# Attention scores on one core: the first set transposed in twelve pieces, and the later twelve output tiles stored two by two

## The chip, the cores and the metric

The kernel runs on one core of a Trainium2 chip. The metric is the device time of one execution in microseconds, given as the median of several executions. A profile is one further execution, recorded instruction by instruction; its own time stands beside its span (from the first to the last recorded instruction) in the table below.

The core has four engines that appear in this text: TensorE (PE in the profile, PEld for its weight loads), VectorE (DVE), ScalarE (ACT) and GpSimd (POOL). SyncE (SP) computes nothing here; its queue (SPq) issues transfers. Transfers (DMA) are carried by 16 engines of their own, called lanes here.

## The reference

```python
def setup_inputs():
    batch, heads, seq, dim = 8, 8, 512, 64
    q, k: float32 [8, 8, 512, 64]

def reference(q, k):
    scale = 1.0 / np.sqrt(q.shape[-1])
    return (np.einsum('bhqd,bhkd->bhqk', q, k) * scale).astype(np.float32)
```

Sixty-four products of 512x64 by 64x512 are formed. The inputs are 16.8 MB together, the float32 output is 67.1 MB, so most of what moves is output.

## The kernel before

**Tiles.** The output is cut into 16 tiles of 4 MB (`ALL = 16`, index `g`). A tile lives in one of four SBUF buffers, `bigs[g % 4]`, each 128 partitions by 2 halves `x` by 8 rows `i` by 512 columns in float32. A tile is made in four quarters, numbered `n = 0..3`: quarter `n` is half `x = n // 2`, rows `i = 0..3` (low) or `4..7` (high). One quarter is four matmuls, each 128x512, into four of the eight PSUM banks `ps[:, i]`, followed by one 128x2048 instruction that multiplies by the scale and writes PSUM to the buffer. The low quarters always use banks 0 to 3 and the high ones banks 4 to 7, so quarter 2 has to wait until quarter 0 has been read out, and quarter 3 until quarter 1 has.

**Sets.** Two consecutive tiles, `2b` and `2b + 1`, use one set `b` of transposed operands. `kT` and `qz` have room for two sets, `b % 2`. A set is made by VectorE from `xb` with two transposes of keys (`turn_keys`, 64x1024) and four of queries (`turn_queries`, 32x1024). Before it makes set `b`, VectorE waits until TensorE has finished with set `b - 2` (`pe >= 8 * (b - 1)`, line 183).

**Loads and casts.** The inputs arrive in seven 2 MB loads and two of 1 MB, into the same four `bigs` buffers that later hold output. GpSimd casts them to bfloat16 into `xb` (line 113), one unit `v` of four after the other, and gives `ready` one count for each cast half-unit.

**Who waits for what.** All order is set by semaphores that are written out by hand; there is no scheduler at work.

- TensorE runs one loop of four iterations over tiles `t = 0..3` (lines 123 to 148). The dictionary `waits` says ahead of which matmul `(x, i)` it waits, and `takes` lowers a semaphore again. A tile's second matmul, `(0, 1)`, waits until the buffer is free. The last matmuls of every second tile, from `(1, 6)` on, wait for the next set: `waits[1, 6] = (f"set{1 - two}", 1)` (line 135).
- ScalarE reads out all 64 quarters in order (lines 151 to 156) and gives `act0`/`act1`, or `out` for a tile's last quarter.
- SyncE, in order, waits for `out`, gives `freed0`/`freed1` to TensorE, and issues the 4 MB store (lines 82 to 88). Each buffer has a semaphore of its own, `store0` to `store3`, which the 16 lanes raise by one each when their share of the store has landed.

Of the kernel before, what the change touches and what calls it, by code (L numbers as in the profile page):

```python
# [5 lines left out]
def kernel(  # L6
# [5 lines left out]
    nc = tc.nc  # L12
    B, H, S, D = q.shape
    scale = 1.0 / (D ** 0.5)
    P = 128
    Q = 32
    UNITS = B // 2
    G = H // 2
# [3 lines left out]
    RO = 8  # L22
    JJ = J // RO
    W = 4
    ALL = 2 * B
    SETS = 2 * UNITS
    SLOTS = UNITS - 1

    f32 = mybir.dt.float32
# [1 line left out]

    names = ["ready", "zeroed", "turned", "pe", "out", "act0", "act1", "freed0", "freed1", "set0", "set1"]
    sem = {name: nc.alloc_semaphore(name) for name in names}
    load_sems = [nc.alloc_semaphore(f"load{n}") for n in range(2 * UNITS)]
    halves = [load_sems[0], nc.alloc_semaphore("load0b")]
    store_sems = [nc.alloc_semaphore(f"store{n}") for n in range(UNITS)]

# [1 line left out]
    q_r = q.rearrange("(v b) (x s h) (m j) d -> v (s h m) (b x) (j d)", b=2, x=2, s=2, j=R)  # L43
    k_r = k.rearrange("(v b) (x s h) (m j) d -> v (s h m) (b x) (j d)", b=2, x=2, s=2, j=R)
    k_0 = k.rearrange("(v b) (x s h) (m j) d -> v b (s h m) x (j d)", b=2, x=2, s=2, m=Q)[0]
    out_r = out.rearrange("(v b) (x s h) (u i) k -> v s b (h u) x (i k)", b=2, x=2, s=2, i=RO)


    bigs = [nc.alloc_sbuf_tensor(f"big{n}", [P, 2, RO, S], f32)[:] for n in range(UNITS)]
    xb = nc.alloc_sbuf_tensor("xb", [P, 2 * SLOTS, J, D, 2], bf16)[:]  # L50
    kT = nc.alloc_sbuf_tensor("kT", [P, 2 * G, S], bf16)[:]
    qz = nc.alloc_sbuf_tensor("qz", [P, 2 * G, RO, P], bf16)[:]
    ps = nc.alloc_psum_tensor("ps", [P, RO, S], f32)[:]

    xw = xb.rearrange("p n w d e -> p n (w d e)").bitcast(f32).rearrange(
        "p n (w d) -> p n w d", d=D)
    kw = kT.bitcast(f32)
    qw = qz.bitcast(f32)

    def xf(v):  # L60
        return bigs[v].rearrange("p x i k -> p (x i k)").rearrange("p (x s c) -> p x s c", x=2, s=2)

    def slot(v, x):
        return v % SLOTS * 2 + x
# [3 lines left out]
    for s, queue in enumerate((nc.sync, nc.scalar)):  # L68
        first_load = queue.dma_start(
            out=xf(0)[:, 0, s].rearrange("p (x c) -> p x c", x=2), in_=k_0[s]  # L70
# [4 lines left out]

    for n in range(1, 2 * UNITS):
        v, x = divmod(n, 2)
        nc.sync.dma_start(out=xf(v)[:, x].rearrange("p s c -> p (s c)"), in_=(k_r, q_r)[x][v]  # L80
                          ).then_inc(load_sems[n], 16)
    for g in range(ALL):
        nc.sync.wait_ge(sem["out"], g + 1)
        if g < ALL - 1:
            nc.sync.sem_inc(sem[f"freed{g // 2 % 2}"], 1)  # L85
        nc.sync.dma_start(out=out_r[g // 4, g // 2 % 2, g % 2],
                          in_=bigs[g % UNITS].rearrange("p x i k -> p x (i k)")
                          ).then_inc(store_sems[g % UNITS], 16)
    for n in range(UNITS):
        nc.sync.wait_ge(store_sems[n], 16)  # L90

    for v in range(UNITS):
        if v == SLOTS:
            nc.gpsimd.wait_ge(sem["turned"], 1)
            nc.gpsimd.sem_inc(sem["set1"], 1)
        for x in range(2):
            if v or x:
                nc.gpsimd.wait_ge(load_sems[2 * v + x], 16)  # L100
            for s in range(2):
                if v == x == 0:
                    nc.gpsimd.wait_ge(halves[s], 16)
                src = xf(v)[:, x, s]
                dst = xb[:, slot(v, x)]
                if x == 0:
                    src = src.rearrange("p (w e d) -> p w e d", e=2, d=D)
                    dst = dst[:, s * J // 2:(s + 1) * J // 2].rearrange("p w d e -> p w e d")
                else:
                    src = src.rearrange("p (jj e i d) -> p jj e i d", e=2, i=RO, d=D)  # L110
                    dst = dst.rearrange("p (i jj) d e -> p jj e i d", i=RO)[
                        :, s * JJ // 2:(s + 1) * JJ // 2]
                cast = nc.gpsimd.tensor_copy(out=dst, in_=src)  # L113
            cast.then_inc(sem["ready"], 1)
        nc.gpsimd.wait_ge(sem["ready"], 2 * v + 2)
        nc.gpsimd.sem_inc(store_sems[v], 16)

# [1 line left out]
    pe = nc.tensor  # L121
    pe.wait_ge(sem["set0"], 1)
    with pe.Fori(0, ALL // 4):
        for t in range(4):
            two, r = divmod(t, 2)
            was = (t + 3) % 4
            waits = {(0, 0): (f"act{was // 2}", was % 2 * 3 + 3), (0, 1): (f"store{t}", 16),
                     (0, W): (f"freed{was // 2}", was % 2 + 1),
                     (1, 0): (f"act{two}", 3 * r + 1), (1, W): (f"act{two}", 3 * r + 2)}
            takes = {(1, 1): (f"store{t}", 16)}  # L130
            if r == 0:
                takes |= {(0, 5): (f"act{1 - two}", 6), (0, 6): (f"freed{1 - two}", 2),
                          (1, 2): (f"set{two}", 1)}
            else:
                waits[1, 6] = (f"set{1 - two}", 1)
            every = sem | {f"store{n}": store_sems[n] for n in range(UNITS)}
            for x in range(2):
                for i in range(RO):
                    if (x, i) in waits:
                        name, count = waits[x, i]  # L140
                        pe.wait_ge(every[name], count)
                    ins = pe.matmul(out=ps[:, i], lhsT=qz[:, 2 * t + x, i], rhs=kT[:, 2 * t + x],  # L142
                                    start=True, stop=True)
                    if i % W == W - 1:
                        ins.then_inc(sem["pe"], 1)
                    elif (x, i) in takes:
                        name, count = takes[x, i]
                        ins.then_inc(every[name], -count)


    for g in range(ALL):
        for n in range(4):
            x, i = n // 2, n % 2 * W
            nc.scalar.wait_ge(sem["pe"], 4 * g + n + 1)
            freed = nc.scalar.mul(out=bigs[g % UNITS][:, x, i:i + W], in_=ps[:, i:i + W], mul=scale)  # L155
            freed.then_inc(sem["out" if n == 3 else f"act{g // 2 % 2}"], 1)

    def turn_keys(b, y):  # L160
        s = b % 2 * 2 * Q
        out = kw[2 * y * Q:2 * (y + 1) * Q, b % 2 * G:(b % 2 + 1) * G]
        if b < 2:
            out = out.rearrange("d g (m w) -> d g w m", m=Q)
        else:
            out = out.rearrange("d g (m w) -> d w m g", w=J)
        return nc.vector.transpose(  # L167
            out=out, in_=xw[s:s + 2 * Q, slot(b // 2, 0), :, y * Q:(y + 1) * Q])

    def turn_queries(b, y, h):  # L170
        s = (b % 2 * 2 + h) * Q
        d = (2 * y + h) * Q
        return nc.vector.transpose(  # L173
            out=qw[d:d + Q, b % 2 * G:(b % 2 + 1) * G, :, h * Q:(h + 1) * Q].rearrange(
                "d g i (m jj) -> d i jj m g", jj=JJ),
            in_=xw[s:s + Q, slot(b // 2, 1), :, y * Q:(y + 1) * Q].rearrange(
                "p (i jj) d -> p i jj d", i=RO))

    nc.vector.memset(qz, 0.0).then_inc(sem["zeroed"], 1)  # L179
    nc.vector.wait_ge(sem["zeroed"], 1)  # L180
    for b in range(SETS):
        if b >= 2:
            nc.vector.wait_ge(sem["pe"], 8 * (b - 1))
        if b % 2 == 0:
            nc.vector.wait_ge(sem["ready"], b + 1)
        for y in range(2):
            last = turn_keys(b, y)
            if b == 0:
                last.then_inc(sem[("act1", "freed1")[y]], (6, 2)[y])
        if b % 2 == 0:  # L190
            nc.vector.wait_ge(sem["ready"], b + 2)
        for y in range(2):
            for h in range(2):
                last = turn_queries(b, y, h)
        last.then_inc(sem["turned" if b == 1 else f"set{b % 2}"], 1)
    nc.vector.sem_inc(sem["set0"], 1)


# [28 lines left out]
```

## Time and profile before

| quantity | value |
|---|---|
| time, median of 10 executions | 200.9 us (200.72 to 201.04) |
| the profiled execution: its time, and its span | 200.76 us, 199.2 us |
| TensorE busy | 86.0 us, 256 matmuls |
| VectorE busy | 99.3 us |
| ScalarE busy | 116.3 us, 64 quarters read out |
| GpSimd busy | 38.9 us |
| HBM read and written | 16.78 MB, 67.11 MB; 421 GB/s over the span |
| granted TensorE clock, mean | 0.807 of full speed |

The profile's busy times are sums over the whole span, and no engine reaches 60% of it. The row of the DMA is a different matter: it has its own line of forty slices, and the time from issue to landing of a store contains the time that it stands in its queue. A transfer's landing is the moment at which all of its lanes have raised its semaphore.

### The profile page before, as it was taken

To read this page: it belongs to the slowest core of one execution; us is meant where nothing else is said; L and a number is where in the kernel's file an instruction comes from. 1 tells how busy PE (TensorE), PEld (TensorE's weight loads), DVE (VectorE), ACT (ScalarE), POOL (GpSimd) and SP (SyncE) were. 2 spreads that over 40 slices of the span, in tenths; PEclk is the share of its full clock that TensorE was granted. 3 is DMA by queue.
4 is the path that set the end of the run, shared out by engine and by line. 5 is a ranking of instruction groups with operands and counts; after the bars stand their busy time and mean duration, and the time that the engine had idled before them with its cause. 6 is when DMAs were issued, how large, how long until landed. Compare 5 with 4: busy or idle time off the path is not lost.

```text
span 199.2 us, 742 instructions
## 1 busy us (share of the span) xinstructions
PE 86.0 (43%) x256; PEld 24.4 (12%) x256; DVE 99.3 (50%) x49; ACT 116.3 (58%) x65; POOL 38.9 (20%) x20
## 2 busy tenths in 40 slices
PE   0000076555566557556555555566657672000000
PEld 0000021111111111111111111121212120000000
DVE  4247999799699599139904990598000000000000
ACT  2000039999999949594959595949595959000000
POOL 0499999797000000000000000000000000000000
PEclk9999999999999966696979797858585869555555
DMA  5999999999999999999999999999999999999997
GB/s 204 428 454 434 428 421 421 421 415 431 434 434 421 438 428 434 434 421 434 431 438 434 420 434 434 428 434 424 431 438 424 438 424 434 434 425 424 421 424 316
DMA packets 5905, 83.90 MB, mean 421 GB/s; under 512 B 400, under 2 KB 400, under 8 KB 912
## 3 DMA queue, kind: packets, MB, share of 16 engines
q1 hardware_dynamic: 5632, 82.84, 97.6%
q10 hardware_dynamic: 272, 1.05, 1.3%
q14 instruction: 1, 0.01, 0.0%
HBM read 16.78 MB, written 67.11 MB: 421 GB/s over the span
## 4 chain that ended last, share of the span: by engine, by line
DMA 49%; ACT 24%; DVE 4%; PE 4%; POOL 2%; issue 0%; SPq 0%
DMA out_dram<-big 43%; ACT big L155 24%; DMA big<-in_q_dram 6%; DVE qz L173 4%; PE ps L142 4%; POOL xb L113 2%; SPq L85 0%
## 5 line engine op out<-in xcount | busy, mean ns | idle before, releaser
L155 ACT ACTIVATE big<-ps 128x2048 f32<-128x2048 f32 x64 | 115.0, 1910 | 50.7 <-PE ps L142 50.6
L142 PE MATMUL ps<-kT,qz 128*128 128x512 bf16 x256 | 86.0, 474 | 80.5 <-DVE qz L173 26.2
L173 DVE STREAM_TRANSPOSE qz<-xb 32x1024 f32<-32x1024 f32 x32 | 64.5, 2015 | 1.5 <-POOL xb L113 1.1
L167 DVE STREAM_TRANSPOSE kT<-xb 64x1024 f32<-64x1024 f32 x16 | 31.3, 1959 | 34.9 <-PE ps L142 28.3
L142 PEld LDWEIGHTS ps<-kT,qz 128*128 128x128 bf16 x256 | 24.4, 112 | 141.6 <-ACT big L155 55.1
L113 POOL CAST xb<-big 128x2048 bf16<-128x2048 f32 x16 | 38.6, 2475 | 9.3 <-DMA big<-in_k_dram 7.5
L179 DVE MEMSET qz<- 128x4096 uint32 x1 | 3.5, 3472 | 2.9 <-PEq L74 2.9
L155 ACT ACT_TABLE_LOAD x1 | 1.3, 1283 | 2.0 <-PEq L74 2.0
L211 POOL MEMSET const-float32-0.0<- 128x1 f32 x1 | 0.1, 98 | 0.2 <-issue 0.2
L211 POOL MEMSET const-bfloat16-1.0<- 128x1 bf16 x1 | 0.1, 101 | 0.0
L211 POOL MEMSET const-uint8-127<- 128x1 uint8 x1 | 0.1, 101 | 0.0
L211 POOL MEMSET const-float32-1.0<- 128x1 f32 x1 | 0.1, 98 | 0.0
## 6 DMA issues: line engine op xcount, KB each, us to landing
out_dram<-big SPq DMA_DIRECT2D x16, 4096.0 KB, 30.1
big<-in_q_dram SPq DMA_DIRECT2D x4, 2048.0 KB, 23.8
big<-in_k_dram SPq DMA_DIRECT2D x3, 2048.0 KB, 23.8
big<-in_k_dram SPq DMA_DIRECT2D x1, 1024.0 KB, 7.1
big<-in_k_dram ACTq DMA_DIRECT2D x1, 1024.0 KB, 8.7
```

What stands on the lines that cost most here:

```text
L113: cast = nc.gpsimd.tensor_copy(out=dst, in_=src)
L142: ins = pe.matmul(out=ps[:, i], lhsT=qz[:, 2 * t + x, i], rhs=kT[:, 2 * t + x], start=True, stop=True)
L155: freed = nc.scalar.mul(out=bigs[g % UNITS][:, x, i:i + W], in_=ps[:, i:i + W], mul=scale)
L167: return nc.vector.transpose(out=out, in_=xw[s:s + 2 * Q, slot(b // 2, 0), :, y * Q:(y + 1) * Q])
L173: return nc.vector.transpose(out=qw[d:d + Q, b % 2 * G:(b % 2 + 1) * G, :, h * Q:(h + 1) * Q].rearrange("d g i (m jj) -> d i jj m g", jj=J ...
L179: nc.vector.memset(qz, 0.0).then_inc(sem["zeroed"], 1)
L211: nc = _bacc.Bacc("TRN2", target_bir_lowering=False, num_devices=1)
```

## The change

Three things change in the order of work, and one in who does it.

1. **The first set in 12 pieces.** Set 0 was made with 2 key and 4 query transposes. It is now made with 4 key transposes (half the heads each) and 8 query transposes (half the rows each). TensorE is released (`set0`) after the first four query pieces, and its high quarters wait for the other four.
2. **The first stores.** Stores of tiles 0 to 2 wait for TensorE (`pe >= 4 * g + 6`, that is, both quarters of the next tile's first half written) in place of ScalarE's `out`, and SyncE gives TensorE no counts for them.
3. **Pairs.** Tiles 4 to 15 are stored two by two: six stores of 8 MB in place of twelve of 4 MB. The four buffers become one tensor `big`, and the semaphores `store0..3` become `free0` and `free1`, one for each pair of buffers. TensorE waits for a free buffer only at the first tile of a pair, for both buffers at once. SyncE gives its count (`high0`/`high1`) once for each pair, after the store is issued.
4. **Quarter 1 by VectorE.** For tiles 4 to 15 quarter 1 is read out by VectorE (`tensor_scalar_mul`, 128x2048 from PSUM), 12 of the 64; ScalarE keeps 52. These 12 stand at fixed places in VectorE's order: for sets 3 to 7, two key transposes, quarter 1 of tile `2b - 2`, two query transposes, quarter 1 of tile `2b - 1`, two query transposes, then the count for the set. The last two tiles' come at the end.

The counts `act` and `freed` become `low` and `high`, one for each half of the PSUM banks.

```diff
-    for g in range(ALL):
-        nc.sync.wait_ge(sem["out"], g + 1)
-        if g < ALL - 1:
-            nc.sync.sem_inc(sem[f"freed{g // 2 % 2}"], 1)
-        nc.sync.dma_start(out=out_r[g // 4, g // 2 % 2, g % 2],
-                          in_=bigs[g % UNITS].rearrange("p x i k -> p x (i k)")
-                          ).then_inc(store_sems[g % UNITS], 16)
+    for g in range(ALL):
+        if g < UNITS - 1:
+            nc.sync.wait_ge(sem["pe"], 4 * g + 6)
+        elif g % 2:
+            nc.sync.wait_ge(sem["out"], (g - UNITS + 3) // 2)
+        else:
+            continue
+        dst = out_r[g // 4, g // 2 % 2]
+        free = sem[f"free{g // 2 % 2}"]
+        if g < UNITS:
+            nc.sync.dma_start(out=dst[:, g % 2 * 2:g % 2 * 2 + 2],
+                              in_=bigs[g].rearrange("p x i k -> p x (i k)")).then_inc(free, 16)
+        else:
+            nc.sync.dma_start(out=dst, in_=big[:, g % UNITS - 1:g % UNITS + 1].rearrange(
+                "p n x i k -> p (n x) (i k)")).then_inc(free, 32)
+        if UNITS - 1 <= g < ALL - 1:
+            nc.sync.sem_inc(sem[f"high{g // 2 % 2}"], 1)
...
-            waits = {(0, 0): (f"act{was // 2}", was % 2 * 3 + 3), (0, 1): (f"store{t}", 16),
-                     (0, W): (f"freed{was // 2}", was % 2 + 1),
-                     (1, 0): (f"act{two}", 3 * r + 1), (1, W): (f"act{two}", 3 * r + 2)}
+            was = (f"{two}", 2) if r else (f"{1 - two}", 4)
+            waits = {(0, 0): ("low" + was[0], was[1]), (0, W): ("high" + was[0], was[1]),
+                     (1, 0): (f"low{two}", 2 * r + 1), (1, W): (f"high{two}", 2 * r + 1)}
             if r == 0:
+                waits[0, 1] = (f"free{two}", 32)
...
             else:
-                waits[1, 6] = (f"set{1 - two}", 1)
+                waits |= {(0, 1): ("ready", 2 * t + 2), (1, 6): (f"set{1 - two}", 1)}
...
+    def evacuate(g, n):
+        x, i = n // 2, n % 2 * W
+        by_vector = g >= UNITS and n == 1
+        engine = nc.vector if by_vector else nc.scalar
+        engine.wait_ge(sem["pe"], 4 * g + n + 1)
+        to, src = bigs[g % UNITS][:, x, i:i + W], ps[:, i:i + W]
+        if by_vector:
+            freed = nc.vector.tensor_scalar_mul(out=to, in0=src, scalar1=scale)
+        else:
+            freed = nc.scalar.mul(out=to, in_=src, mul=scale)
...
+    nc.vector.wait_ge(sem["ready"], 1)
+    for n in range(2):
+        for y in range(2):
+            last = turn_keys(0, y, slice(2 * n, 2 * n + 2))
+    last.then_inc(sem["low1"], 4)
+    nc.vector.wait_ge(sem["ready"], 2)
+    for n in range(RO // W):
+        for y, h in sides:
+            last = turn_queries(0, y, h, slice(n * W, (n + 1) * W))
+        last.then_inc(sem[("set0", "high1")[n]], (1, 4)[n])
+    for b in range(1, SETS):
         if b >= 2:
             nc.vector.wait_ge(sem["pe"], 8 * (b - 1))
         if b % 2 == 0:
             nc.vector.wait_ge(sem["ready"], b + 1)
         for y in range(2):
-            last = turn_keys(b, y)
...
+            turn_keys(b, y)
+        if b > 2:
+            evacuate(2 * b - 2, 1)
         if b % 2 == 0:
             nc.vector.wait_ge(sem["ready"], b + 2)
-        for y in range(2):
-            for h in range(2):
-                last = turn_queries(b, y, h)
+        for n, (y, h) in enumerate(sides):
+            if b > 2 and n == 2:
+                evacuate(2 * b - 1, 1)
+            last = turn_queries(b, y, h)
         last.then_inc(sem["turned" if b == 1 else f"set{b % 2}"], 1)
+    for g in (ALL - 2, ALL - 1):
+        evacuate(g, 1)
     nc.vector.sem_inc(sem["set0"], 1)
```

## The prediction

> **What bounds the kernel now.** I read the page's forty slices first, then the queues, the groups, the chain, and last the instructions in order of time around one landing.
>
> ```profile
> DMA  5999999999999999999999999999999999999997
> GB/s 204 428 454 434 428 421 421 421 415 431 434 434 421 438 428 434 434 421 434 431 438 434 420 434 434 428 434 424 431 438 424 438 424 434 434 425 424 421 424 316
> ...
> q1 hardware_dynamic: 5632, 82.84, 97.6%
> q10 hardware_dynamic: 272, 1.05, 1.3%
> ```
>
> A slice is 4.98 us. Only the first and the last have a lane that waits. The two queues' packets fill 98.9% of 16 lanes over 199.2 us, 197.0 us; what is left is the time ahead of the first byte. So the lanes bound the kernel from end to end, and a change can only win what they idle (about 2 us, nearly all at the start) or lose by letting them run dry.
>
> ```profile
> L155 ACT ACTIVATE big<-ps 128x2048 f32<-128x2048 f32 x64 | 115.0, 1910 | 50.7 <-PE ps L142 50.6
> L173 DVE STREAM_TRANSPOSE qz<-xb 32x1024 f32<-32x1024 f32 x32 | 64.5, 2015 | 1.5 <-POOL xb L113 1.1
> L167 DVE STREAM_TRANSPOSE kT<-xb 64x1024 f32<-64x1024 f32 x16 | 31.3, 1959 | 34.9 <-PE ps L142 28.3
> ...
> out_dram<-big SPq DMA_DIRECT2D x16, 4096.0 KB, 30.1
> ```
>
> A store needs 30.1 us from issue to landing, though one follows another every 9.8 us: some twenty of the thirty are spent behind two other stores. That queue is the cover of everything else. The chain shows one round of it:
>
> ```profile
> 56.66 25.07 DMA out_dram<-big
> 81.73 0.05 issue
> 81.78 1.47 PE ps L142 x3
> 83.25 0.02 issue
> 83.27 7.19 ACT big L155 x4
> 90.47 0.02 issue
> 90.48 0.02 SPq L85
> 90.50 0.05 issue
> 90.55 30.44 DMA out_dram<-big
> ```
>
> A landing at 81.73 frees a buffer; the tile is issued at 90.55, 8.8 us later; two more stores are then still ahead of it. TensorE at that landing, and at the one before:
>
> ```profile
> 71.99 3.17 PE L142 MATMUL ps<-kT,qz 128*128 128x512 bf16 x7 [2.59 <-DMA out_dram<-big]
> 75.42 3.07 PE L142 MATMUL ps<-kT,qz 128*128 128x512 bf16 x8 [0.26 <-ACT big L155]
> ...
> 81.78 3.06 PE L142 MATMUL ps<-kT,qz 128*128 128x512 bf16 x7 [2.10 <-DMA out_dram<-big]
> 85.20 1.04 PE L142 MATMUL ps<-kT,qz 128*128 128x512 bf16 x4 [0.37 <-ACT big L155]
> ```
>
> Seven matmuls after a wait take 3.1 to 3.2 us, four later ones 1.04 us.
>
> **What the Trainium skill says.** "TensorE: Matmul & The Clock Gate", part 1, gives N = 512 matmuls 427 ns cold and 216 ns warm, after some 3.4 us of work or of idling; the trace agrees in kind (0.45 and 0.26 us apiece, above). "VectorE: DVE Perf Modes", "Why PSUM operands drop a tier", says that float32 read from PSUM runs at one element a cycle; no row here shows it. "DMA: Bandwidth & Descriptors", "Anatomy of one DMA", calls the semaphore write at a transfer's end nearly free; the trace agrees, as its packet records show the 16 lanes full across every store boundary.
>
> **The change part by part.**
>
> *Twelve pieces.* Six transposes of 2.0 us become twelve of about half that; if each pays 0.1 us of its own, VectorE loses 0.6 us, while TensorE may start after half the queries, 4 us earlier. Tile 0 ends about 2 us earlier; tile 3 still waits for GpSimd's last casts at 48.5 us, as before. What hides both signs is the queue of loads, which keeps the lanes full until 42 us. The first store goes out at 35.4 us now and must by about 40. Cost: nothing. If the cover were gone, it would be worth those 2 us.
>
> *The first stores' wait.* Store `g` goes out after the next tile's first eight matmuls, about 1.2 us after ScalarE's last quarter. Stores 0 to 2 are issued near 34.7, 42 and 51 us; the lanes reach them at 42, 52 and 61. Behind SyncE's wait stand only later stores. Cost: nothing, by 7 us or more.
>
> *ScalarE's relief.* Twelve quarters of 1.88 us leave it, 23 us. It waits 50.7 us for TensorE already; worth nothing by itself.
>
> *Pairs.* Six boundaries disappear; gain about nothing, see above. What changes is the cover: where two or three stores stood ahead of a new one, there is now exactly one, of 8 MB. A pair cannot start before both of its buffers have landed, and its store must be delivering when the other pair runs out. Landings 1 and 3 lie at 62.22 and 81.73 us, 19.51 apart; the packet records show the lanes running out between 80.76 and 81.30, mean 81.03. So from landing 62.22 to new bytes there are **18.8 us**.
>
> *What has to fit in them* (pair of tiles 4 and 5; times from the landing). The fixed place of quarter 1 in VectorE's order, together with the old wait at `(1, 6)` for the next set, makes one serial chain:
>
> - 0.05 to 3.2: TensorE resumes, seven cold matmuls (3.1 to 3.2). Quarter 1 is ready.
> - 3.25 to 5.5: VectorE reads it out. The same page's cycle table ("The TRN2 errata") has 120 + FD cycles from PSUM at 0.96 GHz: 2168 cycles, 2.26 us, an estimate. The nearest row, ScalarE's same tile at 1.88, is the lower bound I believe in; two elements a cycle would be 1.2. I take 2.26.
> - 5.5 to 9.55: two query transposes, 2 x 2.01.
> - The second tile's quarter 1 needs ScalarE's quarter 3 of the first tile read out. TensorE writes that quarter after 5.55 (four matmuls, 1.04 warm or 1.7 cold), ScalarE takes 1.88, TensorE four more matmuls: ready at 9.65 warm, 11.0 cold.
> - VectorE reads it (2.26): 11.9 or 13.3.
> - Two more query transposes, then the set's count, +4.05 and 0.1: 16.05 or 17.45. Only now may TensorE do the tile's last two matmuls (0.55 or 0.85): 16.6 or 18.3.
> - ScalarE's last quarter, 1.9: 18.5 or 20.2. SyncE's wait and issue, 0.07: 18.6 or 20.3.
> - First bytes: the first load was issued at 0.73 us and its first packet stands at 1.86, 1.13 later; over a store's lanes I add 0.35. Together 1.48: 20.1 or 21.8.
>
> Against 18.8 the lanes idle **1.3 to 3.0 us**. The wait before a pair is some 3 us, so the first matmuls are cold and the middle partly warm: I take 1.8. The two transposes and the wait at `(1, 6)` stood in the old kernel too, and were covered.
>
> *How often.* The stall is late next at the other pair, but helps it: pair 6/7 starts from landing 3, not later, with the same 19.5 us ahead plus the 1.8 by which the store in front of it is late. So it just fits. Pair 8/9 starts from the late landing of 4/5 and again falls short. Short: 4/5, 8/9 and 12/13; fitting: 6/7, 10/11 and 14/15 (which makes no set). Three times 1.8 is 5.4; 0.2 for jitter in those that just fit.
>
> *Other waits.* VectorE's key transposes of the next set (3.9 us) begin when the last matmul of a pair is done, 18 us at worst, and end 22 us after its landing, which is 2.5 us after the next; quarter 1 needs VectorE at 3.2. SyncE's count for the high banks comes after the issue, near 20 us, and is needed at 21. Both are hidden, narrowly.
>
> **Sum.** 200.76 us (span 199.2 and 1.56 around it) + 5.4 + 0.2 = 206.4; the profiled execution lies 0.14 under the median of the runs, so 206.5.
>
> **The rivals.**
>
> *The chain is shorter and hidden, no change.* It must lose 1.3 us or more even warm: VectorE at two elements a cycle (2 x 1.06 less), or first bytes half a microsecond sooner with warm matmuls. The page on VectorE speaks against the first. Then 200.8. Chance 0.09, of which 0.02 leaves a small loss.
>
> *Faster.* The slices alternate near 438 and 424 GB/s; if those dips were store boundaries, each would cost 14/438 x 4.98 = 0.16 us, and six fewer 1.0: 199.9. It decides only where the chain fits in 17.3 us up to the issue. The full lanes in the packet records speak against dips. Chance 0.03.
>
> *Short at every pair.* If the key transposes or SyncE's late count hold up the pairs that I let fit, five or six stalls, and 10 or 11 us: near 211. For it: margins of 1 us or less in cold rounds. Against: the 1.8 us that the pair in front is late. Chance 0.08.
>
> **How the numbers follow.** My forecast has 0.80. Its own range comes from 3 x 0.6 (VectorE at 1.88 us) to 3 x 3.0: 202.5 to 209.5. Below lie the first two rivals, above the third, together 0.20, so this is also the range for the time. A difference under 0.2% is about what a measurement of this kernel can tell from no change; within it 0.07, faster 0.03, slower 0.80 + 0.08 + 0.02 = 0.90.
>
> **What would show it.** The DMA row should drop below 9 in three slices, near 81, 122 and 162 us, and GB/s there by a third. SyncE's six long waits should end on ScalarE's last quarter, and before that TensorE should wait for VectorE's query transposes, 3 to 4 us in each of tiles 5, 7, 9, 11 and 13. VectorE's new row should read 2.2 to 2.3 us. I am wrong if that wait is short, if the row is near 1.2, or if the lanes stay full; wrong in size if the DMA stalls come at other than three places.

## The result, and the profile after

The changed kernel takes **205.77 us** (median of 9, 204.29 to 206.6) against 200.9 us: ratio 1.0224, 95% interval 1.0208 to 1.024. The profiled execution takes 203.96 us over a span of 202.4 us, 3.2 us more than the profiled execution before; it is faster than any of the nine, and a later section comes back to that.

First the page's slices and queues, and the groups that answer to those of before:

```profile
DMA  6999999999999999899999999999899999999998
GB/s 205 449 434 414 421 456 418 414 414 443 421 431 437 427 427 418 363 450 431 414 414 414 414 413 411 421 414 414 363 414 421 460 388 440 414 414 437 443 414 363
...
q1 hardware_dynamic: 5536, 82.84, 96.6%
q10 hardware_dynamic: 272, 1.05, 1.3%
...
L174 ACT ACTIVATE big<-ps 128x2048 f32<-128x2048 f32 x52 | 95.0, 1880 | 80.2 <-PE ps L156 80.2
L200 DVE STREAM_TRANSPOSE qz<-xb 32x1024 f32<-32x1024 f32 (+1 forms) x36 | 65.0, 1807 | 1.2 <-POOL xb L127 0.7
L172 DVE TENSOR_SCALAR big<-ps 128x2048 f32<-128x2048 f32 x12 | 27.5, 2292 | 29.2 <-PE ps L156 29.2
...
out_dram<-big SPq DMA_DIRECT2D x6, 8192.0 KB
```

The queues' packets now fill 97.9% of 202.4 us, 198.1 us, where they filled 197.0 of 199.2: the same work within 1.1 us, and more room around it. Apart from the last slice, two show an 8 and 363 GB/s, at 81 to 86 us and at 142 to 147 us; smaller gaps vanish in a slice's mean. From the trace's packet records I counted how many of the 16 lanes carry a packet at each moment and summed what was missing:

| new pair | lanes dry from (us) | mean idle (us), profiled execution |
|---|---|---|
| 4/5 | 80.8 | 0.82 |
| 6/7 | 101.4 | 0.34 |
| 8/9 | 121.4 | 0.65 |
| 10/11 | 141.7 | 1.07 |
| 12/13 | 162.4 | 0.22 |
| 14/15 | | 0 |

That is 3.1 us, against 0.1 us in the kernel before over the same part, and so nearly the whole difference of 3.2 us. Two smaller terms cancel: the packets took 1.1 us longer (above), and at the two ends of the run the lanes were idle 1.1 us less. Here is pair 4/5, from the landing that frees its buffers to its store, as instructions in order of time (start, duration, engine, instruction, idle before it and its releaser):

```profile
62.35 3.17 PE L156 MATMUL ps<-kT,qz 128*128 128x512 bf16 x7 [5.74 <-DMA out_dram<-big]
...
65.56 2.29 DVE L172 TENSOR_SCALAR big<-ps 128x2048 f32<-128x2048 f32 x1 [6.20 <-PE ps L156]
67.77 4.02 DVE L200 STREAM_TRANSPOSE qz<-xb 32x1024 f32<-32x1024 f32 x2
71.99 2.29 DVE L172 TENSOR_SCALAR big<-ps 128x2048 f32<-128x2048 f32 x1 [0.20 <-PE ps L156]
74.31 3.99 DVE L200 STREAM_TRANSPOSE qz<-xb 32x1024 f32<-32x1024 f32 x2
...
78.36 0.82 PE L156 MATMUL ps<-kT,qz 128*128 128x512 bf16 x3 [3.42 <-DVE qz L200]
...
79.00 1.88 ACT L174 ACTIVATE big<-ps 128x2048 f32<-128x2048 f32 x1 [3.37 <-PE ps L156]
...
80.91 0.44 SPq L99 DMA_DIRECT2D out_dram<-big  x1
```

Each step begins within 0.1 us of the end of the one before, but for VectorE's wait of 0.20 us. From 65.56 to 78.30 it is busy without another pause. TensorE waits 3.42 us for its transposes in the middle of the pair's last quarter (the third matmul at 78.36 is the next pair's first), then ScalarE's quarter waits, then the store. From the landing at 62.30 to the issue there are 18.6 us; the lanes run out at 81.04 on average and new packets begin at 81.82 to 81.96. In the four later pairs that stall the same stretch takes 19.05 to 19.53 us.

### The profile page after: what moved, and what is told of

It reads as the page before. It is cut to its first block, busy times and chain, and to the rows that moved or that the text cites. A ratio compares the mean times of both kernels' runs of the same rounds, so it can differ in the third digit from the quotient of the medians.

```text
span 202.4 us, 730 instructions
## 1 busy us (share of the span) xinstructions
PE 84.7 (42%) x256; PEld 23.4 (12%) x256; DVE 127.2 (63%) x67; ACT 96.3 (48%) x53; POOL 38.9 (19%) x20
## 3 DMA queue, kind: packets, MB, share of 16 engines
q10 hardware_dynamic: 272, 1.05, 1.3%
## 4 chain that ended last, share of the span: by engine, by line
DMA 39%; ACT 16%; DVE 16%; PE 8%; POOL 7%; issue 2%; POOLq 0%
DMA out_dram<-big 33%; ACT big L174 16%; DVE qz L200 12%; PE ps L156 8%; POOL xb L127 7%; DMA big<-in_q_dram 6%; DVE big L172 2%; DVE kT L195 1%; POOLq L111 0%
## 5 line engine op out<-in xcount | busy, mean ns | idle before, releaser
L174 ACT ACTIVATE big<-ps 128x2048 f32<-128x2048 f32 x52 | 95.0, 1880 | 80.2 <-PE ps L156 80.2
L156 PE MATMUL ps<-kT,qz 128*128 128x512 bf16 x256 | 84.7, 467 | 91.7 <-DVE qz L200 42.3
L200 DVE STREAM_TRANSPOSE qz<-xb 32x1024 f32<-32x1024 f32 (+1 forms) x36 | 65.0, 1807 | 1.2 <-POOL xb L127 0.7
L172 DVE TENSOR_SCALAR big<-ps 128x2048 f32<-128x2048 f32 x12 | 27.5, 2292 | 29.2 <-PE ps L156 29.2
L156 PEld LDWEIGHTS ps<-kT,qz 128*128 128x128 bf16 x256 | 23.4, 111 | 152.5 <-ACT big L174 41.9
L195 DVE STREAM_TRANSPOSE kT<-xb 64x1024 f32<-64x1024 f32 (+1 forms) x18 | 31.6, 1754 | 14.8 <-PE ps L156 8.1
```

Source lines behind the costliest of these rows:

```text
L172: freed = nc.vector.tensor_scalar_mul(out=to, in0=src, scalar1=scale)
L174: freed = nc.scalar.mul(out=to, in_=src, mul=scale)
L195: return nc.vector.transpose(out=out, in_=src)
L200: return nc.vector.transpose(out=qw[d:d + Q, b % 2 * G:(b % 2 + 1) * G, rows, h * Q:(h + 1) * Q].rearrange("d g i (m jj) -> d i jj m g", j ...
```

## The experiments

The theory is this serial chain. One rival is that the pairs are slow in themselves: 8 MB transfers, their layout, or only one store of cover. The other is that VectorE reads PSUM more slowly than ScalarE (2.29 against 1.88 us, above), whatever it waits for.

**The wait moved.**

```diff
-                waits |= {(0, 1): ("ready", 2 * t + 2), (1, 6): (f"set{1 - two}", 1)}
+                waits |= {(0, 1): ("ready", 2 * t + 2)}
...
                 for i in range(RO):
+                    if r == x == i == 0:
+                        pe.wait_ge(sem[f"set{two}"], 1)
                     if (x, i) in waits:
```

> The wait for the next set moves from the last two matmuls of a pair to the first matmul of the next pair; nothing else changes. Theory (the serial chain through VectorE's order and that wait): the last quarter of a pair starts about 4 us earlier, a pair is issued some 15 us after its landing and not 18.6 or more, no lane runs dry: 200.9 us, within 0.4. Rival pairs (8 MB stores with one of cover, or their layout, are slow in themselves): stays near 205.8. Rival VectorE (it reads PSUM more slowly than ScalarE and that alone lengthens a tile): stays near 205.8, or loses at most the 1 us that the two quarters differ by.

Measured: 200.66 us (20 executions), ratio to the kernel before 0.9988 (0.9981 to 0.9995). Its slices, and TensorE and SyncE in order of time around pair 6/7:

```profile
DMA  6999999999999999999999999999999999999997
...
98.64 0.61 PE L158 MATMUL ps<-kT,qz 128*128 128x512 bf16 x1 [3.00 <-DVE qz L202]
101.64 2.74 PE L158 MATMUL ps<-kT,qz 128*128 128x512 bf16 x6 [2.39 <-DMA out_dram<-big]
...
97.69 0.40 SPq L99 DMA_DIRECT2D out_dram<-big  x1
```

TensorE still waits 3.00 us for the same transposes. But the wait is now behind the pair: its store is issued at 97.69, ahead of the set's end at 98.6, and 15.5 us after the landing at 82.2. No lane runs dry. VectorE's twelve quarters and the six 8 MB stores are all still there, so both rivals fall as causes of the loss.

**All quarters by ScalarE.**

```diff
-        by_vector = g >= UNITS and n == 1
+        by_vector = False
...
-            if g < UNITS or n != 1:
-                evacuate(g, n)
+            evacuate(g, n)
...
-        if b > 2:
-            evacuate(2 * b - 2, 1)
...
-            if b > 2 and n == 2:
-                evacuate(2 * b - 1, 1)
...
-    for g in (ALL - 2, ALL - 1):
-        evacuate(g, 1)
```

> ScalarE reads out all 64 quarters again; pairs, twelve pieces and the wait for the set stay. Theory: VectorE makes the next set without a stop, some 12 us after the landing at the latest, the wait is covered, ScalarE's eight quarters bound the pair (1.5 + 8 x 1.8 = 16 us from landing to issue): just fits, 200.9 us, at most 202 if the matmuls are cold. Rival pairs: stays near 205.8. Rival VectorE: 200.9.

Measured: 200.4 us (10 executions), ratio 0.9979 (0.9969 to 0.9988). ScalarE and SyncE in order of time:

```profile
83.49 14.27 ACT L174 ACTIVATE big<-ps 128x2048 f32<-128x2048 f32 x8 [5.17 <-PE ps L156]
...
97.78 0.40 SPq L99 DMA_DIRECT2D out_dram<-big  x1
```

Eight quarters run through in 14.27 us without a stop; the issue is 15.8 us after the landing at 81.94. The relief of ScalarE was not needed: with 64 quarters it is done sooner than with 52 and a partner that has other work.

**Single stores.** `free0` to `free3`, one for each buffer, in place of two; the store of every tile in 4 MB.

```diff
         elif g % 2:
             nc.sync.wait_ge(sem["out"], (g - UNITS + 3) // 2)
         else:
-            continue
+            nc.sync.wait_ge(sem["pe"], 4 * g + 6)
...
-        free = sem[f"free{g // 2 % 2}"]
+        free = sem[f"free{g % UNITS}"]
...
-                waits[0, 1] = (f"free{two}", 32)
+                waits[0, 1] = (f"free{t}", 16)
```

> The later tiles are stored one by one in 4 MB again, each buffer with its own semaphore; VectorE's twelve quarters, their places and the wait for the set stay. Theory: the chain is as long as before, but two or three stores stand ahead of every tile, so that it is covered: 200.9 us. Rival pairs: 200.9. Rival VectorE: between 200.9 and 205.8, as its slower quarters stay.

Measured: 200.84 us (12 executions), ratio 0.9999 (0.999 to 1.0008). Slices, and TensorE in order of time:

```profile
DMA  5999999999999999999999999999999999999996
...
91.60 2.27 PE L152 MATMUL ps<-kT,qz 128*128 128x512 bf16 x6 [3.42 <-DVE qz L196]
```

The wait of 3.42 us is in place, to the hundredth, and costs nothing. So the loss needs both: a chain that lasts as long as the one store ahead of it, and the loss of the other stores as cover. The size of the stores and the number of semaphores change together here; which of the two takes the cover away is not separated.

**One query transpose moved forward.**

```diff
-        if b > 2:
-            evacuate(2 * b - 2, 1)
...
-            if b > 2 and n == 2:
-                evacuate(2 * b - 1, 1)
+            if b > 2 and n in (1, 3):
+                evacuate(2 * b - 2 + n // 2, 1)
```

> VectorE's order alone changes: for sets 3 to 7 one query transpose stands ahead of each of the two quarters and one behind each, so that one and not two lie between the second quarter and the set's count. The wait for the set, VectorE's twelve quarters and the pairs stay. Theory: the chain loses 2.0 us, at worst 1.5 because the first quarter may wait for the transpose in front of it; the stalls of 0.2 to 1.1 us vanish: 200.7 us, within 0.4. Rivals (pairs or VectorE slow in themselves): 205.8.

Measured: 200.77 us (20 executions), ratio 0.9991 (0.9985 to 0.9998). TensorE and VectorE in order of time:

```profile
96.02 0.82 PE L156 MATMUL ps<-kT,qz 128*128 128x512 bf16 x3 [1.42 <-DVE qz L200]
...
81.56 2.01 DVE L200 STREAM_TRANSPOSE qz<-xb 32x1024 f32<-32x1024 f32 x1
85.21 2.29 DVE L172 TENSOR_SCALAR big<-ps 128x2048 f32<-128x2048 f32 x1 [1.64 <-PE ps L156]
```

The wait shrinks from 3.42 to 1.42 us, the 2.0 of one transpose, and the moved one fits in time in which VectorE was idle: after it there are still 1.64 us to spare. The order alone, with every instruction and wait kept, undoes the loss.

**Two transposes more.** Two query transposes go to a spare tile, ahead of the count.

```diff
             last = turn_queries(b, y, h)
+        if b > 2:
+            for n in range(2):
+                last = nc.vector.transpose(
+                    out=spare[n * Q:(n + 1) * Q].rearrange("d (g i m jj) -> d i jj m g", g=G, i=RO, jj=JJ),
+                    in_=xw[:Q, slot(b // 2, 1), :, :Q].rearrange("p (i jj) d -> p i jj d", i=RO))
```

> Two query transposes of 2.0 us into a spare tile are added ahead of the count for each of sets 3 to 7. Theory as forecast, with a stall at every second pair (4/5, 8/9, 12/13): 3 x 4.0 more, near 218. If instead each of the five pairs pays it: 5 x 4.0 more, near 226. Rivals pairs and VectorE, in which the wait for the set is not last: no more than 1 us over 205.8.

Measured: 218.09 us (4 executions, 217.4 to 220.81); without the longest of them the ratio is 1.0845 (1.0815 to 1.0874). The number is the forecast one, but not for the reason given. Slices, and TensorE, VectorE in order of time:

```profile
DMA  6999999999999990999679996999499959999998
...
131.58 3.68 PE L157 MATMUL ps<-kT,qz 128*128 128x512 bf16 x8 [0.16 <-SPq L103]
...
124.07 3.98 DVE L237 STREAM_TRANSPOSE spare<-xb 32x1024 f32<-32x1024 f32 x2
129.18 3.90 DVE L196 STREAM_TRANSPOSE kT<-xb 64x1024 f32<-64x1024 f32 x2 [1.13 <-PE ps L157]
133.50 2.29 DVE L173 TENSOR_SCALAR big<-ps 128x2048 f32<-128x2048 f32 x1 [0.42 <-PE ps L157]
```

There are five stalls: 5.54, 3.43, 2.57, 2.70 and 2.53 us by the packet records. From the landing to the issue of pair 4/5 there are now 23.0 us (62.77 to 85.78), more than the 19.5 between two landings, so a pair's landing comes before the pair ahead is through. The rounds of compute then follow each other directly (VectorE's first quarters start at 111.31, 133.50 and 155.79, 22.2 apart), TensorE waits for SyncE's late count as well, and each pair from the third on pays about 22.2 less the 19.6 that its store takes. Agreement in the sum does not show the pattern.

**Half a transpose more**, to ask for the pattern where the chain still ends near the next landing: the same edit with one 32x512 transpose.

> One half query transpose (1.1 us, as the first set's pieces measured) into a spare tile is added ahead of the count for each of sets 3 to 7. Forecast's step that the stall comes at every second pair: 3 x 1.1 = 3.3 more than 205.8, 209.1. The step's rival, each of the five pairs pays: 5 x 1.1 = 5.5 more, 211.3. Lanes' records should show three large stalls, or five like ones.

Measured: 207.51 us (4 executions, 207.16 to 208.76), ratio 1.0349 (1.0322 to 1.0376); 1.7 us over the changed kernel by medians, 3.2 by the profiled executions (207.16 and 203.96). Slices:

```profile
DMA  6999999999999997899999987999799989999998
GB/s 196 447 424 436 424 433 424 427 417 433 420 446 420 443 424 309 341 424 408 459 408 408 449 365 334 433 408 459 306 459 408 430 376 417 411 455 408 433 433 357
```

Dry lanes: 2.61, 0.18, 1.67, 1.10 and 0.76 us, 6.3 in all. Neither of the two pictures holds as drawn, and neither number was met. A pair starts from its own landing, whatever the other pair has lost meanwhile, so a stall and the one ahead of it together make up what one pair falls short: 2.61 for the first, then 2.79, 1.85, 2.77 and 1.86. The larger ones follow a landing whose counts are spread over 0.9 to 1.1 us from the first lane to the last, the two smaller ones a landing within 0.14 us. Five stalls thus cost about three payments: the growth of the profiled executions is near the 3.3 us of three, that of the medians lies under it, and both stay under the 5.5 of five.

**Pairs with six pieces.** The kernel of the second experiment, with set 0 in six transposes again and TensorE released after the last.

```diff
-    for n in range(2):
-        for y in range(2):
-            last = turn_keys(0, y, slice(2 * n, 2 * n + 2))
+    for y in range(2):
+        last = turn_keys(0, y)
...
-    for n in range(RO // W):
-        for y, h in sides:
-            last = turn_queries(0, y, h, slice(n * W, (n + 1) * W))
-        last.then_inc(sem[("set0", "high1")[n]], (1, 4)[n])
+    for y, h in sides[:3]:
+        turn_queries(0, y, h)
+    turn_queries(0, *sides[3]).then_inc(sem["high1"], 4)
+    nc.vector.wait_ge(sem["high1"], 4)
+    nc.vector.sem_inc(sem["set0"], 1)
```

> Pairs and the new first stores alone: ScalarE reads out all quarters, and the first set is made in six transposes as before the change, TensorE released after the last. Theory (the twelve pieces are hidden behind the loads, worth nothing): as with twelve pieces, 200.4 us. Rival (the gain of 0.4 us of that kernel comes from the earlier start): back to 200.85.

Measured: 200.42 us (12 executions), ratio 0.9976 (0.9967 to 0.9985), as with twelve pieces. The pieces are worth nothing. This version and that of the second experiment are faster than the kernel before by 0.2%, and both intervals lie under 1.

**The changed kernel, profiled twice more.**

> The changed kernel, unaltered, for a second profiled execution: its profile of 203.96 us lies 1.8 us under its own median. Theory (the forecast's cold end: where more matmuls fall into half-clock stretches, the second tile's quarter 1 comes later and the chain grows): a slower execution shows a lower granted clock, more idle lanes in the same five places by just the difference in time, and VectorE waiting longer for the second tile's quarter. Rival (something outside the pairs, such as the loads or the program's end): the same 3.1 us of idle lanes, the difference elsewhere.

> A third profiled execution of the changed kernel, for the same question and with the same expectations as the second.

Measured: 205.71 us at a granted clock of 0.774, and 203.97 us at 0.788 (the first profile: 203.96 at 0.797). The first of the two is the median case. Its slices, and TensorE, VectorE, SyncE for pair 4/5:

```profile
DMA  6999999999999998899999988999899989999998
...
65.88 1.86 PE L156 MATMUL ps<-kT,qz 128*128 128x512 bf16 x4 [0.26 <-ACT big L174]
...
72.55 2.29 DVE L172 TENSOR_SCALAR big<-ps 128x2048 f32<-128x2048 f32 x1 [0.69 <-PE ps L156]
...
78.93 1.46 PE L156 MATMUL ps<-kT,qz 128*128 128x512 bf16 x3 [3.42 <-DVE qz L200]
...
81.91 0.44 SPq L99 DMA_DIRECT2D out_dram<-big  x1
```

The four matmuls after the first seven took 1.04 us in the first profile and take 1.86 here; the second tile's quarter 1 is 0.5 us later for it, and VectorE waits 0.69 us. The three matmuls after the wait of 3.42 us took 0.82 us and take 1.46, which makes ScalarE's last quarter another 0.4 us later. The issue comes 19.5 us after the landing at 62.40. The lanes are dry for 1.80, 0, 1.31, 0.87 and 0.78 us, 4.8 in all: 1.7 more than in the first profile, and 1.75 is what the time grew. In the other, 203.97 us, they are dry for 2.9 us (the five stalls alone 2.8). So the spread of the times is the same chain with more of its matmuls at the slower pace, as far as three executions show. All executions of the changed kernel lean the same way: 203.96 and 204.36 us at a mean granted clock of 0.797, 205.77 at 0.766 and 0.774, 206.6 at 0.750.

## Why the prediction was right or wrong

- **Time.** 206.5 forecast, 205.77 measured; the stalls were to cost 5.6 us and cost 4.8 in the execution nearest the median (205.71 us). The ends of the range, 200.9 + 3 x 0.6 and 200.9 + 3 x 3.0, are 202.7 and 209.9, and not 202.5 and 209.5.
- **The lanes bound the kernel, and a change can only let them run dry:** right. The dry lanes come within 0.3 us of the difference in both the 203.96 and the 205.71 us execution.
- **The chain:** right in every member, in their order: all five waits for the transposes are 3.42 us, and SyncE's six long waits end on ScalarE's last quarter. In the median-like execution its length from landing to issue is 19.5 us, between the two sums of 18.6 and 20.3; in the first profile's pair 4/5 it is the warm sum to 0.1 us. The rival that the chain is hidden fell with the wait of 3.42 us and with the first experiment.
- **VectorE's quarter from PSUM:** 2.26 us estimated from the Trainium skill's "VectorE: DVE Perf Modes", cycle table of the errata; 2.29 measured. One element a cycle holds; two would have been 1.2 us, an estimate by the same table.
- **First bytes after the issue, 1.48 us: the term that was too large.** Measured 0.91 to 1.05 in the first profile (80.91 to 81.82 and 81.96). The 1.48 was taken from the kernel's first load. With 1.0 the range of one stall is 0.8 to 2.5 us; measured in pair 4/5 were 0.82 and 1.80. That the second is the very 1.8 that was taken is luck: the chain was longer than this choice implied (19.5 us against 19.1, which is 18.8 + 1.8 - 1.48), and the first bytes came sooner by about as much.
- **How often: the step that failed in form.** Not three stalls and three that fit, but stalls at five pairs; and as they are smaller, the DMA row drops in two slices and not in three, GB/s there by an eighth (363 against some 415) and not by a third. By the prediction's own sign it was wrong here. The step that the stall is late next at the other pair and helps it is sound (0 at 6/7 in the median-like execution, behind 1.80), and so the five stalls sum to about three payments (1.80, 0 + 1.31 and 0.87 + 0.78 there). That a pair which just fits stays at zero is not sound: it has no slack, so every lengthening of its own chain (18.6 to 19.5 us in the first profile) and every late landing falls on it. The 1.07 us at 10/11 follow a landing in which one lane ended at 122.36 where the mean was 121.51.
- **Twelve pieces at nothing:** right. A query piece takes 1.10 us where half of 2.0 was 1.0, so that VectorE reaches set 1 0.87 us later (27.02 against 26.15 us) and not 0.6; ScalarE starts at 24.53 and not 28.15; the first store is issued at 35.51 and not, as forecast, at 34.7. All of it disappears behind the loads.
- **Six boundaries fewer worth nothing:** right within 0.2 us where VectorE has its twelve quarters. With pairs (the wait moved) 200.66, with single stores 200.84; the lanes' mean end is 197.98 and 198.04 us. With ScalarE alone, pairs and the new first stores are worth 0.5 us (200.42 against 200.95); the last point is about that.
- **VectorE and SyncE hidden narrowly before the next pair:** right for the change, and the experiment with two transposes more shows them uncovered.
- **Not foreseen:** that ScalarE alone, with pairs, beats the kernel before by 0.2%. Half of it is also gained with the wait moved. In the medians of all executions, both have a span of 199.1 us against 199.3 before. The other half lies outside the span: the time less the span is 1.34 us with ScalarE alone (1.31 with six pieces), 1.56 with the wait moved and 1.61 before. What happens in these 0.3 us was not tried.

## What to carry to other kernels

Before transfers are merged, count the stores that stand ahead of a new one, and compare that time with the longest serial path from a landing to the next issue, at the slow end of TensorE's clock. Half the buffers behind one semaphore left 18.8 us for a path that had some 29 (three stores of 9.8), and the path was 18.6 to 19.5 before the first byte. When an engine is lent to relieve another that waits anyway, its own work behind the loan is what comes late: look at the count that it gives last, and put its other work into the wait ahead of the loan rather than behind it.

## What the runs showed of the hardware that was not expected

- A lane that ends 0.8 us after the others costs nothing while more stores are queued (in the kernel before, at 149.9 us against a mean of 149.2, no lane is idle). Where the landing releases the next pair it is paid: with half a transpose more, pairs fell 2.6 to 2.8 us short after a landing spread over 0.9 us or more, and 1.85 and 1.86 us after one within 0.14 us.
- A 16 KB packet takes 611 ns at the median in the 4 MB stores of the kernel before and in the 8 MB stores of the moved wait alike (613 in the changed kernel): the packets of the larger transfer are no faster.
- Between the end of a landing's last packet and TensorE's first matmul there are 0.41 and 0.47 us (81.39 and 81.80 us in the profile after, 81.31 and 81.78 in the one before). Most of it passes before the last count is on record, at 81.75 and 81.73. With first bytes about 0.9 us after an issue, a dependent transfer costs 1.4 us beside the work itself.
